# 640 accumulator columns divided into 512 and 128 in place of 320 and 320

## The chip, the cores and the metric

The kernel runs on one core of one Trainium2 chip. The metric is the device time of one execution in microseconds; the time before is the median of three runs. The profile is that of one further execution.

## What is computed

One inference step of a two-layer trunk on 128 context tokens and 512 latent tokens, 640 in all, model width 1024, in float32. The reference, cut to what matters here:

```python
# layer 0: latent attention || windowed attention
h, gate = _adaln(x, ln, mod)                       # RMSNorm, then h*(1+scale)+shift
cq, ckv, krope, z_a, q_b, k_b, v_b, z_b = _split(h @ w_in, L0_SPLIT)
q_a = (_rms(cq, mla_q_norm) @ w_uq)                # 8 heads of 64 + 32 (rotary)
k_a, v_a = _mla_expand(ckv, krope, w_ukv)          # 640 keys for a latent query
o_a = softmax(q_a k_a^T * MLA_SCALE) v_a           # dense
o_b = windowed softmax with sink                   # |i-j| <= 128, plus 128 cached keys
y = concat(o_a * silu(z_a), o_b * silu(z_b)) @ w_out;  x = x + gate * y

# layer 1: bidirectional gated DeltaNet || dense attention
q, k, v = silu(short_conv(qkv))                    # 3 taps along the tokens, 1536 columns
o_f, o_b = chunked delta rule, forward and backward
o_d = softmax(q_d k_d^T * ATT_SCALE) v_d           # 4 heads, 640 keys for a latent query
y = concat(gated GDN output, o_d * silu(z_d)) @ w_out
```

## The kernel before

Every projection is computed in three passes: each operand is kept as a high part and a low part in the type fp32r (`split`, lines 108 to 111: ScalarE writes the high part, VectorE or GpSimd the low one), and `mm3` (lines 113 to 118) issues high*high, then two mixed products, into one PSUM accumulator. A PSUM bank holds 512 float32 columns.

There are two kinds of projection. `proj_tok` (tokens on the partitions of the result) takes one 128-token tile as the stationary operand and streams up to 512 weight columns; the change does not touch it. `proj_col` (lines 191 to 203; the columns of the weight on the partitions, the tokens along the free dimension) holds a 128x128 block of the weight stationary and streams the tokens. 640 tokens do not fit one bank, so there are two accumulators. For each weight unit (four row blocks), the two accumulators are served one after the other, with 4 x 3 matmuls each. `proj_col` is called 13 times in layer 0 (keys and queries of the windowed attention, `use_qk`; the two gates, `use_z` and `z_raw`) and 16 times in layer 1 (twelve column blocks for the short convolution, `use_conv` with `conv`, lines 1026 to 1037, and four gate blocks, `use_zd`).

The same division of 640 stands at four other places: the rotary part of the latent queries (line 569), `heads_q` (line 711, by `col3`), the scores of the latent attention (line 772; 32 tiles of 128 queries by 640 keys, three passes each) and those of the dense attention of layer 1 (line 1380; 16 tiles). `heads_k` (line 723) covers 768 keys in two accumulators of 384. Scores lie in an accumulator `S` of two banks; `softmax` (line 310) takes the maximum on VectorE (line 319) and the exponential on ScalarE (line 321) over all 640.

The order of each engine's instructions is set when the kernel is built: a scheduler goes through the program with a model of durations and writes one fixed order for each engine. Weights come in on SP's queue (`unit`, line 134), in that order too. The modulation vectors are computed by `gemv_mm` (line 228), whose small matmuls (line 236) read `wmod` tiles just loaded and stand between the projections.

Of the kernel before, what the change touches and what calls it, by code (L numbers as in the profile page):

```python
# [22 lines left out]
NT = 5  # L23
EPS = 1e-6
# [8 lines left out]
class Blocks:  # L33
    """row blocks of an operand of 1024 rows, in two tiles"""
# [11 lines left out]
class Kern:  # L46
    def __init__(self, ctx, tc, io):
        self.ctx, self.tc, self.nc, self.io = ctx, tc, tc.nc, io
        self.n = 0
        self.dve_share = 2      # one in so many evacuations goes to VectorE  # L50
# [25 lines left out]
    def banks(self, ctx, **roles):  # L76
        """PSUM banks by role; role "S2" counts accumulators of two banks"""
# [3 lines left out]
        for r in roles:         # banks in the order of the roles  # L81
            self.acc2() if r == "S2" else self.acc1(r)
# [4 lines left out]
    def acc1(self, role="tr"):  # L87
        if role not in self.roles:      # any bank, in turn
            self.nb = getattr(self, "nb", 0) + 1
            role = ("sc", "tr", "sc", "tr", "sc", "o")[self.nb % 6]  # L90
        return self.t(self.ps, [128, 512], role, bufs=self.roles[role])

    def ranked(self, rank):
        """decorator: what the function issues is scheduled that much earlier (or later)"""
# [51 lines left out]
    def unit_in(self, src, raw, hi, lo, eng):  # L146
        """unit in flat views of tiles at hand"""
# [6 lines left out]
    def proj_tok(self, name, n, hT, use, order="k", us=None, pre=None):  # L154
        """[tokens, n] = h @ w for the five token tiles; units hold as many row blocks as fit 4 KB"""
# [35 lines left out]
    def proj_col(self, src, hT, use):  # L191
        """[128 columns, tokens] in two accumulators of 320 tokens; src [2][128, 4, 128]"""
        hh, hl = hT
        us = [self.unit(src[i], [4, 128]) for i in range(2)]
        ps = [self.acc1("pj")[:, 0:320] for _ in range(2)]
        for i in range(2):
            wh, wl = us[i]
            for f in range(2):
                r = slice(f * 320, f * 320 + 320)
# [28 lines left out]
    def gemv_mm(self, m, src, out):  # L228
        """out [128, 256] (PSUM): partial products of both vectors with src [8][128, 512]; rows 32 (2 (k % 2) + f) + group"""
# [9 lines left out]
    def mod_k(self, m, c):  # L239
        """shift and scale of the row blocks 2 c and 2 c + 1"""  # L240
# [10 lines left out]
        # columns of mt: (f = shift | scale, row block, group)  # L251
# [9 lines left out]
    def mod_gate(self, m, c, role="tr"):  # L261
        """gate, columns 512 c .. 512 c + 511, bias included: two summands by group to DRAM"""
# [11 lines left out]
    def gate(self, m, pool, gt=None):  # L274
        """gates of both groups on all partitions"""
# [8 lines left out]
    def xhat(self, x, junk):  # L284
        """normalises x in place"""
# [7 lines left out]
    def norm_T(self, t, x, m, hT, th):  # L293
        """transposed, modulated x (normalised) of token tile t"""
# [15 lines left out]
    def softmax(self, S, shape, pool, scale, l, tag="P"):  # L310
        """S: PSUM view [128, ...]; returns P in SBUF, flat [128, n], not normalised; sums into the column l"""
# [12 lines left out]
    def factors(self, L, rd, pool, tag="rB", bufs=1):  # L324
        """1 / L [128 tokens, heads x tiles], one row per head, on all partitions of the head's columns; rd [heads x tiles, 128]"""
# [15 lines left out]
    def gated(self, o, z, ts):  # L341
        """gate the values o[:, 0:n] of tokens ts"""
# [11 lines left out]
    def layer0(self, m0, m1):  # L354
# [21 lines left out]
        # normalised, transposed input; modulated row block by row block as the modulation vectors come in  # L376
        xT = [self.t(sw, [128, 4, NTOK], "g10", bufs=2) for _ in range(2)]
        # tiles of later use serve as further buffers here
# [25 lines left out]
        # small operands  # L404
# [20 lines left out]
        def modulate(k):  # L425
            """row block k of the modulated input"""
# [45 lines left out]
        def use_qk(j):  # L472
            def use(ps):
                X = self.t(tmp, [128, NTOK], "tX", bufs=3)
                for f in range(2):
                    self.evac(X[:, f * 320:f * 320 + 320], ps[f])
# [27 lines left out]
        # per key head: both parts of the queries, against keys of which both halves hold the same part  # L504
# [48 lines left out]
        def use_z(z, j):  # L553
            def use(ps):
                for f in range(2):
                    nc.scalar.activation(out=z[:, j, f * 320:f * 320 + 320], in_=ps[f], func=AF.Silu)
# [4 lines left out]
        # ---- rotary part of the latent queries  # L561
# [1132 lines left out]
```

## Time and profile before

| | |
|---|---|
| time, median of 3 runs | 919.71 us (915.09 to 920.54) |
| profiled execution: span from first to last instruction | 909.3 us |
| PE (TensorE matmul) busy | 839.4 us, 92% of the span, 5762 matmuls |
| PEld (weight loads) busy | 708.0 us, 78%, 5762 loads |
| DVE / ACT / POOL busy | 559.9 us (62%) / 374.3 us (41%) / 291.0 us (32%) |
| mean granted TensorE clock | 0.962 |

The page gives no time of the profiled execution beside its span; the median of the timed runs lies 10.4 us above the span, which is what lies before the first and behind the last instruction, and the difference between executions. In the rows of the timeline the columns are the start in us, the duration in us, the engine, the line, the operation, what it writes and reads, the shape and the count. For a matmul the shape names the stationary operand (128\*128) and the result (128x320: 128 partitions, 320 columns). The duration of a single matmul contains the way through the array, so the cost of one in a sequence is read from the distance of two starts, not from its duration.

### The profile page before, as it was taken

The numbers are of one execution on the slowest core, as the hardware profiler recorded it, in microseconds if no ns is written. First come the engines' busy times: TensorE is split into PE (matmuls) and PEld (weight loads), VectorE is DVE, ScalarE is ACT, GpSimd is POOL, SyncE is SP. The second block draws the span as 40 slices with busy tenths as digits, with TensorE's granted clock in tenths as the row PEclk, the third lists the DMA queues.
The fourth block names the chain that finished last, engine by engine and source line by source line (L and its number), as shares of the span: only waits on it lengthen the run. The fifth ranks groups of instructions, "written<-read, shape, count | busy, mean of one in ns | idle before, by whom it ended". The sixth has DMA issues, their size and how long they took to land.

```text
span 909.3 us, 15742 instructions
## 1 busy us (share of the span) xinstructions
PE 839.4 (92%) x5762; PEld 708.0 (78%) x5762; DVE 559.9 (62%) x1260; ACT 374.3 (41%) x916; POOL 291.0 (32%) x398
## 2 busy tenths in 40 slices
PE   5999899989999999999999799999788799999996
PEld 3579779977868776688888679888688688988785
DVE  4546545266476676524986646756997357887634
ACT  5234423345476566513445525342232323456330
POOL 2013434220141013243672101032995012145441
PEclk9899999999999999999999899999898769999999
DMA  9875894230270111364933545449205913346512
GB/s 315 308 230 137 221 305 121 85 82 15 67 188 16 30 30 43 101 235 138 218 111 98 172 139 148 111 148 250 58 25 134 267 52 107 112 123 212 185 47 93
DMA packets 100935, 124.46 MB, mean 137 GB/s; under 512 B 20014, under 2 KB 60698, under 8 KB 100602
## 3 DMA queue, kind: packets, MB, share of 16 engines
q1 hardware_dynamic: 97418, 115.60, 42.8%
q0 software_dynamic: 2720, 5.25, 2.7%
q10 hardware_dynamic: 720, 2.62, 0.7%
q8 instruction: 45, 0.74, 0.3%
q14 instruction: 32, 0.26, 0.1%
HBM read 100.48 MB, written 20.39 MB: 133 GB/s over the span
## 4 chain that ended last, share of the span: by engine, by line
PE 67%; DVE 12%; DMA 10%; ACT 4%; issue 3%; POOL 2%; SPq 1%; DVEq 0%; ACTq 0%; POOLq 0%
PE pj L116 10%; PE pj L117 10%; PE pj L118 10%; PE tr L122 6%; PE S L772 3%; PE o L796 2%; DVE Ub L1167 2%; DVE wb L1165 2%; PE tr L236 2%; PE S L1380 1%; PE o L659 1%; PE sc L1282 1%; DMA wmod<-in_w_mod 1%; PE sc L1230 1%; PE sc L117 1%
## 5 line engine op out<-in xcount | busy, mean ns | idle before, releaser
L110 ACT ACTIVATE whi<-wraw 128x512 fp32r<-128x512 f32 (+4 forms) x113 | 75.1, 666 | 184.0 <-PE pj L118 53.1
L111 DVE TENSOR_TENSOR wlo<-wraw,whi 128x512 fp32r<-128x512 f32 (+3 forms) x76 | 59.6, 785 | 79.6 <-ACT whi L110 77.6
L111 POOL TENSOR_TENSOR wlo<-wraw,whi 128x512 fp32r<-128x512 f32 (+4 forms) x37 | 50.9, 1375 | 142.7 <-ACT whi L110 121.9
L116 PE MATMUL pj<-hUh,whi 128*128 128x320 f32 x256 | 81.8, 319 | 0.8 <-DVE Ub L1167 0.6
L118 PE MATMUL pj<-hUh,wlo 128*128 128x320 f32 x256 | 81.3, 317 | 1.3 <-DVE wlo L111 1.3
L117 PE MATMUL pj<-hUl,whi 128*128 128x320 f32 x256 | 81.5, 318 | 0.0
L116 PE MATMUL pj<-hTh,whi 128*128 128x320 f32 x208 | 66.2, 318 | 3.9 <-ACT whi L110 3.9
L117 PE MATMUL pj<-hTl,whi 128*128 128x320 f32 x208 | 66.1, 318 | 0.0
L118 PE MATMUL pj<-hTh,wlo 128*128 128x320 f32 x208 | 65.7, 316 | 0.0
L116 PE MATMUL pj<-whi,hUh 128*128 128x512 f32 (+2 forms) x160 | 57.1, 358 | 9.1 <-DVE t L931 6.1
L117 PE MATMUL pj<-wlo,hTh 128*128 128x512 f32 (+1 forms) x160 | 59.5, 374 | 0.0
L319 DVE TENSOR_REDUCE smx<-S 128x1 f32<-128x640 f32 (+1 forms) x60 | 42.6, 713 | 26.3 <-PE S L772 10.5
L116 PE MATMUL pj<-whi,hTh 128*128 128x512 f32 (+1 forms) x160 | 57.7, 374 | 0.9 <-ACT Xs L131 0.9
L118 PE MATMUL pj<-whi,hTl 128*128 128x512 f32 (+1 forms) x160 | 57.2, 368 | 0.0
L118 PE MATMUL pj<-whi,hUl 128*128 128x512 f32 (+2 forms) x160 | 55.9, 352 | 0.4 <-DVE hUl L111 0.4
L321 ACT ACTIVATE P<-S,smx 128x640 f32<-128x640 f32 (+1 forms) x60 | 42.4, 708 | 33.0 <-DVE smx L320 31.3
L117 PE MATMUL pj<-wlo,hUh 128*128 128x512 f32 (+2 forms) x160 | 55.8, 349 | 0.0
L116 PEld LDWEIGHTS pj<-hUh,whi 128*128 128x128 f32 x256 | 49.2, 192 | 5.8 <-issue 4.5
L118 PEld LDWEIGHTS pj<-hUh,wlo 128*128 128x128 f32 x256 | 49.4, 193 | 2.0 <-DVE wlo L111 1.6
L117 PEld LDWEIGHTS pj<-hUl,whi 128*128 128x128 f32 x256 | 49.2, 192 | 1.3 <-issue 1.2
L116 PEld LDWEIGHTS pj<-hTh,whi 128*128 128x128 f32 x208 | 39.7, 191 | 5.7 <-ACT whi L110 4.1
L116 PEld LDWEIGHTS pj<-whi,hUh 128*128 128x128 f32 x160 | 31.8, 199 | 13.1 <-DVE t L931 6.6
(529 smaller groups left out, 2249.8 us busy)
## 6 DMA issues: line engine op xcount, KB each, us to landing
Pw<-in_w_mod SPq DMA_DIRECT2D x48, 256.0 KB
wraw<-in_w1c SPq DMA_DIRECT2D x32, 256.0 KB
wraw<-in_w_out SPq DMA_DIRECT2D x16, 512.0 KB
wraw<-in_w0c SPq DMA_DIRECT2D x26, 256.0 KB
zB<-in_w_mod SPq DMA_DIRECT2D x16, 256.0 KB
zA<-in_w_mod SPq DMA_DIRECT2D x16, 256.0 KB
wmod<-in_w_mod SPq DMA_DIRECT2D x16, 256.0 KB
ut_d<-zt SPq DMA_DIRECT2D x10, 258.0 KB
```

What stands on the lines that cost most here:

```text
L110: self.last_hi = nc.scalar.activation(out=hi, in_=src, func=AF.Copy)
L111: (lo_eng or nc.vector).tensor_tensor(out=lo, in0=src, in1=hi.bitcast(F32), op=ALU.subtract)
L116: nc.tensor.matmul(out, ah, bh, start=start, stop=False)
L117: nc.tensor.matmul(out, ah, bl, start=False, stop=False)
L118: nc.tensor.matmul(out, al, bh, start=False, stop=stop)
L122: self.nc.tensor.transpose(out, in_, self.ident[:p, :p])
L236: nc.tensor.matmul(out[32 * g:32 * g + 32, 0:256], self.sc[:, k, :], raw[:, f * 256:(f + 1) * 256], start=(k < 2), stop=(k >= 6), tile_pos ...
L319: nc.vector.tensor_reduce(out=m, in_=src, axis=AX.X if len(shape) == 1 else AX.XY, op=ALU.max)
L321: nc.scalar.activation(out=Pv, in_=src, func=AF.Exp, bias=nm, scale=scale, accum_out=l)
L772: nc.tensor.matmul(S[:, f, 0:320], Qe[:, a, qs], Ke[:, b, 128 + 320 * f:448 + 320 * f], start=(a + b == 0), stop=(a == 1))
L796: nc.tensor.matmul(o[rr[e], 0:256], V[:, 1 + s, hc[e]], x[:, e * 256:(e + 1) * 256], start=(s == 0), stop=(s == 4), tile_position=(0, 64 * e))
L1165: eng.tensor_tensor(out=w, in0=Ub[:, r, c:c + 1].to_broadcast([80, nr, nn]), in1=Lb[d][:, c:c + 1, cc].to_broadcast([80, nr, nn]), op=ALU. ...
```

## The change

640 tokens or keys are divided into 512 and 128. In the column projections, `SEG` serves the 512 latent tokens (128 to 639) first and the 128 context tokens behind them. In the scores the first 512 keys fill one bank of `S` and the other 128 the start of the next, so that the 640 scores lie contiguous. `heads_k` divides its 768 into 512 and 256. `conv` copies its input with two instructions in place of three, since the boundary of the segments is now the boundary between the token groups. The number of matmuls and of multiplied columns stays the same. The rest of the diff removes comments.

```diff
+SEG = (slice(128, 640), slice(0, 128))
...
     def proj_col(self, src, hT, use):
         us = [self.unit(src[i], [4, 128]) for i in range(2)]
-        ps = [self.acc1("pj")[:, 0:320] for _ in range(2)]
+        ps = [self.acc1("pj")[:, 0:r.stop - r.start] for r in SEG]
         for i in range(2):
             wh, wl = us[i]
-            for f in range(2):
-                r = slice(f * 320, f * 320 + 320)
+            for f, r in enumerate(SEG):
                 for k in range(4):
                     kk = 4 * i + k
                     self.mm3(ps[f], (wh[:, k, :], wl[:, k, :]), (hh[:, kk, r], hl[:, kk, r]), kk == 0, kk == KD - 1)
...
-                    self.evac(X[:, f * 320:f * 320 + 320], ps[f])
+                    self.evac(X[:, SEG[f]], ps[f])
...
-            for f in range(2):
-                r = slice(f * 320, f * 320 + 320)
-                ps = self.acc1("pj")[:, 0:320]
+            for r in SEG:
+                ps = self.acc1("pj")[:, 0:r.stop - r.start]
...
-        def col3(w, cols, x, nk, half, use, wide=False):
+        def col3(w, cols, x, nk, segs, use, wide=False):
-            for f in range(2):
+            for r in segs:
...
-            col3(uk, slice(j * 128, j * 128 + 128), ckT, 2, 384, use_k, j == 0)
+            col3(uk, slice(j * 128, j * 128 + 128), ckT, 2, (slice(0, 512), slice(512, 768)), use_k, j == 0)
...
-                        S = self.acc2()
+                        S = self.acc2().rearrange("p a b -> p (a b)")
                         for (a, b) in ((0, 0), (0, 1), (1, 0)):
                             for f in range(2):
-                                nc.tensor.matmul(S[:, f, 0:320], Qe[:, a, qs], Ke[:, b, 128 + 320 * f:448 + 320 * f],
+                                nc.tensor.matmul(S[:, 512 * f:512 + 128 * f], Qe[:, a, qs], Ke[:, b, 128 + 512 * f:640 + 128 * f],
                                                  start=(a + b == 0), stop=(a == 1))
-                        Ps[q, e] = self.softmax(S[:, :, 0:320], [2, 320], pp, MLA_SCALE, Ls[j % 2][:, NT * e + q + 1:NT * e + q + 2])
+                        Ps[q, e] = self.softmax(S[:, 0:640], [640], pp, MLA_SCALE, Ls[j % 2][:, NT * e + q + 1:NT * e + q + 2])
...
         def conv(ps, c):
-            nc.scalar.copy(xp[:, 1:129], ps[0][:, 0:128])
-            nc.vector.tensor_copy(xp[:, 130:322], ps[0][:, 128:320])
-            nc.scalar.copy(xp[:, 322:642], ps[1])
+            nc.scalar.copy(xp[:, 130:642], ps[0])
+            nc.vector.tensor_copy(xp[:, 1:129], ps[1])
...
-                        nc.tensor.matmul(S[:, f, 0:320], qD[a][:, h, qs], kD[b][:, g, 128 + 320 * f:448 + 320 * f],
+                        nc.tensor.matmul(S[:, 512 * f:512 + 128 * f], qD[a][:, h, qs], kD[b][:, g, 128 + 512 * f:640 + 128 * f],
                                          start=(a + b == 0), stop=(a == 1))
-                Ps.append(self.softmax(S[:, :, 0:320], [2, 320], pp, ATT_SCALE, L[:, 1 + q:2 + q]))
+                Ps.append(self.softmax(S[:, 0:640], [640], pp, ATT_SCALE, L[:, 1 + q:2 + q]))
```

The scheduler writes new orders with it. The line numbers of the changed kernel lie one above or below those of before (`mm3` is lines 117 to 119, a load line 107, the scores of the latent attention line 771). Two places follow.

On PE, the first scores of the latent attention (tile `S`) stood before as six equal matmuls, two accumulators in each of three passes:

```order
L118 MATMUL pj_3299<-cqTh_248,hTh_529_2696 128x320
L772 MATMUL S_628_3123<-K_537_2716,Q_533_2712 128x320 x6
```

Now they alternate between 512 and 128 columns:

```order
L771 MATMUL S_628_3123<-K_537_2716,Q_533_2712 128x512
L771 MATMUL S_628_3123<-K_537_2716,Q_533_2712 128x128
L771 MATMUL S_628_3123<-K_537_2716,Q_533_2712 128x512
L771 MATMUL S_628_3123<-K_537_2716,Q_533_2712 128x128
L771 MATMUL S_628_3123<-K_537_2716,Q_533_2712 128x512
L771 MATMUL S_628_3123<-K_537_2716,Q_533_2712 128x128
```

So no two long matmuls follow each other within a tile of scores; in the column projections 12 or 24 long ones are followed by as many short ones.

On SP, in layer 1 between the first column projections, the loads of `wmod` (modulation), of `wraw` (weights) and the store and re-load of the decay exponents (`gc_d`, then `Dm` on all partitions) stood before in this order:

```order
L106 DMA wmod_5489<-in_w_mod 128x512
L106 DMA wmod_5493<-in_w_mod 128x512
L106 DMA wraw_5878<-in_w1c 128x512
L106 DMA gc_d_4840<-gcT_5175 40x128
L106 DMA Dm_5178<-gc_d_4840 128x5x128 x2
L106 DMA Dm_5192<-gc_d_4840 128x5x128 x2
L106 DMA wmod_5497<-in_w_mod 128x512
```

They now stand in this one (the numbers of the `wmod` and `wraw` tiles are three to six lower in the changed kernel):

```order
L107 DMA gc_d_4840<-gcT_5175 40x128
L107 DMA wmod_5486<-in_w_mod 128x512
L107 DMA Dm_5178<-gc_d_4840 128x5x128 x2
L107 DMA Dm_5192<-gc_d_4840 128x5x128 x2
L107 DMA wmod_5490<-in_w_mod 128x512
L107 DMA wraw_5872<-in_w1c 128x512
```

The store of the exponents has moved ahead of two modulation loads and one weight load, and its re-load ahead of one of each.

More of the change, by code (lines that the diff above doesn't have):

```diff
@@ L555, in use @@
                 for f in range(2):
-                    nc.scalar.activation(out=z[:, j, f * 320:f * 320 + 320], in_=ps[f], func=AF.Silu)
+                    nc.scalar.activation(out=z[:, j, SEG[f]], in_=ps[f], func=AF.Silu)
             return use
@@ L678, in use @@
                 for f in range(2):
-                    self.evac(zA[:, j, f * 320:f * 320 + 320], ps[f])
+                    self.evac(zA[:, j, SEG[f]], ps[f])
             self.proj_col(io["w0c"][9 + j], hT, use)
@@ L701, in mla_setup @@
                 self.load(K[b][1][32:64], krd, nc.gpsimd)
-        def col3(w, cols, x, nk, half, use, wide=False):
-            for f in range(2):
-                ps = (self.acc2()[:, 0, 0:half] if wide else self.acc1("pj")[:, 0:half])
+        def col3(w, cols, x, nk, segs, use, wide=False):
+            for r in segs:
+                n = r.stop - r.start
+                ps = (self.acc2()[:, 0, 0:n] if wide else self.acc1("pj")[:, 0:n])
                 for k in range(nk):
-                    r = slice(f * half, f * half + half)
                     self.mm3(ps, (w[0][:, k, cols], w[1][:, k, cols]), (x[0][:, k, r], x[1][:, k, r]), k == 0, k == nk - 1)
-                use(slice(f * half, f * half + half), ps)
+                use(r, ps)
         def heads_q(j):
@@ L718, in use_q @@
                     self.split(ps[p], Qj[e][p, 0, r], Qj[e][p, 1, r])
-            col3(uq[j // 2], slice((j % 2) * 128, (j % 2) * 128 + 128), cqT, 3, 320, use_q, j == 0)
+            col3(uq[j // 2], slice((j % 2) * 128, (j % 2) * 128 + 128), cqT, 3, SEG, use_q, j == 0)
             for e in range(2):
@@ L1194, in use @@
                 for f in range(2):
-                    nc.scalar.activation(out=zz[:, f * 320:f * 320 + 320], in_=ps[f], func=AF.Silu)
+                    nc.scalar.activation(out=zz[:, SEG[f]], in_=ps[f], func=AF.Silu)
                 self.load(zd_d[j], zz)
@@ L1375, in scores @@
             for q in range(4):
-                S = self.acc2()
+                S = self.acc2().rearrange("p a b -> p (a b)")
                 qs = slice(128 + 128 * q, 256 + 128 * q)
```

## The prediction

> **What bounds the kernel now.** I read the busy times first, then the chain that ended last, then the table of stages, then starts in the timeline.
>
> ```profile
> PE 839.4 (92%) x5762; PEld 708.0 (78%) x5762; DVE 559.9 (62%) x1260; ACT 374.3 (41%) x916; POOL 291.0 (32%) x398
> PE 67%; DVE 12%; DMA 10%; ACT 4%; issue 3%; POOL 2%; SPq 1%; DVEq 0%; ACTq 0%; POOLq 0%
> PE pj L116 10%; PE pj L117 10%; PE pj L118 10%; PE tr L122 6%; PE S L772 3%; PE o L796 2%; DVE Ub L1167 2%; DVE wb L1165 2%; PE tr L236 2%; PE S L1380 1%; PE o L659 1%; PE sc L1282 1%; DMA wmod<-in_w_mod 1%; PE sc L1230 1%; PE sc L117 1%
> ```
>
> TensorE is busy for 92% of the span and carries 67% of the chain; the three lines of `mm3` alone carry 30%. PEld has as many weight loads as there are matmuls: no load is shared, also where two matmuls in a row have the same stationary operand. The average hides stages with other limits, so here are the stages that hold affected matmuls (start:end, length, then PE, PEld, DVE, ACT and POOL busy, clock, DMA share, GB/s):
>
> ```profile
> 96.00:275.00 179.00, 169.20 (x1193) 143.35 (x1194) 94.39 (x223) 79.67 (x203) 49.62 (x48) 0.99 0.47 132
> 275.00:375.00 100.00, 98.55 (x660) 75.78 (x658) 65.70 (x148) 60.04 (x138) 20.97 (x17) 1.00 0.09 28
> 450.00:510.00 60.00, 49.89 (x338) 43.99 (x337) 45.97 (x124) 29.36 (x83) 26.75 (x59) 0.94 0.48 133
> 510.00:545.00 35.00, 35.00 (x242) 29.63 (x241) 17.12 (x28) 13.55 (x35) 4.43 (x13) 1.00 0.45 135
> 545.00:585.00 40.00, 38.04 (x251) 36.40 (x250) 27.18 (x66) 18.23 (x42) 5.75 (x14) 1.00 0.45 130
> 625.00:716.00 91.00, 77.94 (x541) 71.00 (x539) 74.83 (x182) 25.34 (x81) 61.67 (x112) 0.91 0.47 118
> 716.00:830.00 114.00, 107.63 (x1101) 97.87 (x1102) 80.08 (x201) 47.12 (x136) 30.84 (x28) 0.88 0.39 113
> ```
>
> From 96 to 375 us PE is busy for 95% of the time or more, and from 510 to 545 us without a gap. Two stages are different, as the chain cut to 450 to 510 us and to 625 to 716 us shows:
>
> ```profile
> by line: DMA wmod<-in_w_mod 16.2%; issue 15.6%; POOL t L942 5.9%; PE pj L236 5.3%; POOL t L932 4.5%; POOL th L306 4.2%; PE pj L117 3.9%; PE pj L116 3.8%; DVE wlo L111 3.7%; PE pj L118 3.4%; DVE t L1035 3.4%; PE tr L122 2.5%; POOL ssq L128 2
> by line: DVE Ub L1167 23.7%; DVE wb L1165 23.1%; SPq L106 6.4%; DMA Dm<-L_d 5.3%; DMA U<-ut_d 5.2%; DMA ut_d<-LA 4.5%; DVE wlo L111 4.5%; issue 4.4%; DVE t L940 3.7%; DVE t L931 3.3%; DMA wraw<-in_w1c 2.8%; PE pj L116 1.5%; DVE vDl L111 1.5
> ```
>
> In the first, `mm3` has 11% of the chain, between DMA and the normalisation on POOL; in the second the inversion of the blocks on DVE (L1165, L1167) holds 47%. PE idles 10.1 and 13.1 us there.
>
> **What one pair costs.** The change replaces each pair of 320-column matmuls by one of 512 and one of 128. The number of instructions and of columns stays, so everything hangs on the cost of a matmul by its length. In an undisturbed column projection of before, the first and the last of 24:
>
> ```profile
> 182.96 0.31 PE L116 MATMUL pj<-hTh,whi 128*128 128x320 f32 x1
> ...
> 186.33 0.31 PE L118 MATMUL pj<-hTh,wlo 128*128 128x320 f32 x1
> ```
>
> 23 distances in 3.37 us: 147 ns for 320 columns. In a token projection, the first and the last of 20 with 512 columns:
>
> ```profile
> 399.69 0.39 PE L117 MATMUL pj<-wlo,hTh 128*128 128x512 f32 x1
> ...
> 404.00 0.39 PE L118 MATMUL pj<-whi,hTl 128*128 128x512 f32 x1
> ```
>
> 19 distances in 4.31 us: 227 ns. Short ones of the same type stand in the scores of the context tokens and between long ones in the mask of the windowed attention:
>
> ```profile
> 302.13 0.28 PE L117 MATMUL S<-K,Q 96*128 96x128 f32 x1
> 302.24 0.27 PE L118 MATMUL S<-K,Q 96*128 96x128 f32 x1
> ...
> 181.60 0.39 PE L621 MATMUL S<-kB0h,g 128*128 128x512 f32 x1
> 181.82 0.33 PE L623 MATMUL S<-mask,identR 128*128 128x128 f32 x2
> 181.99 0.45 PE L624 MATMUL S<-kB0l,g 128*128 128x512 f32 x1
> 182.28 0.40 PE L621 MATMUL S<-kB1h,g 128*128 128x512 f32 x1
> ```
>
> The first two rows lie 110 ns apart. From 181.60 to 182.28 two matmuls of 512 and two of 128 take 0.68 us; less 2 x 227 this leaves 113 ns for a short one, in company of long ones. From 320 to 512 columns a column costs (227 - 147) / 192 = 0.42 ns, which would make 128 columns 67 ns. The short ones cost 112: something other than the streaming of columns sets their pace, and with one weight load for each matmul I take it for that load, which 147 ns of streaming cover and 67 do not. A new pair then costs 227 + 112 = 339 ns where the old one cost 2 x 147 = 294: **45 ns more for each pair**. Bounds from the rows: 67 ns for the short one gives no change (294), 113 gives 46.
>
> The Trainium skill weighs the other way: its page "TensorE: Matmul & The Clock Gate", section "Back-to-back issue gap", gives an isolated matmul N / 2.4 + 2.5 ns, which counts columns alone: 216 + 56 = 272 ns for the new pair and 2 x 136 = 272 for the old, so a change of nothing. By the rows above it is 45 ns. The trace does not agree with that formula for 128 columns (56 against 112), though the same section warns that it leaves out the weight load.
>
> **How many pairs, and where.** 29 column projections of 24 pairs are 696; the rotary part has 18, `heads_q` 4 x 9 = 36, the scores 32 x 3 = 96 and 16 x 3 = 48: 894 pairs. `heads_k` goes from 384 + 384 to 512 + 256, both long enough, and I cost it at nothing. So PE gets 894 x 45 ns = **40 us** more work. By stage, from the rows of one of the three passes (for 96 to 275, 450 to 510, 510 to 545, 545 to 585, 625 to 716 and 716 to 830 us, the last from a score's pass):
>
> ```profile
> L116 PE MATMUL pj<-hTh,whi 128*128 128x320 f32 x192 | 61.2, 319 | 3.9 <-ACT whi L110 3.9
> L116 PE MATMUL pj<-hUh,whi 128*128 128x320 f32 x70 | 22.6, 323 | 0.2 <-DVE t L931 0.2
> L116 PE MATMUL pj<-hUh,whi 128*128 128x320 f32 x57 | 18.2, 320 | 0.0
> L116 PE MATMUL pj<-hUh,whi 128*128 128x320 f32 x65 | 20.3, 312 | 0.0
> L116 PE MATMUL pj<-hUh,whi 128*128 128x320 f32 x64 | 20.7, 323 | 0.6 <-DVE Ub L1167 0.6
> L1380 PE MATMUL S<-kDh,qDh 128*128 128x320 f32 x30 | 8.9, 380 | 1.5 <-ACT P L321 1.5
> ```
>
> Three passes, two matmuls to a pair: a row of x192 is 288 pairs.
>
> - 96 to 275 us: 288 pairs, with the rotary part and the first `heads_q` some 318: 14.3 us. PE is busy for 169.2 of 179 us, so 95% of it counts: 13.5.
> - 275 to 375 us: 96 pairs of scores and about 23 of `heads_q`: 5.4 us, all of it.
> - 450 to 510 us: 105 pairs, 4.7 us. PE idles 10.1 us for others: 0.
> - 510 to 545 us: 86 pairs, 3.9 us, all.
> - 545 to 585 us: 98 pairs, 4.4 us. PE is nearly full, but the chain also leads through the decay masks; half: 2.2.
> - 625 to 716 us: 96 pairs of the last gate blocks and 3 of scores, 4.5 us, beside the inversion on DVE: 0. If that cover were gone, all 4.5 would count.
> - 716 to 830 us: 45 pairs of scores, 2.0 us, 94% busy: 1.9.
> - The 24 pairs before 96 us (1.1 us) lie where DMA and the modulation decide: 0.
>
> The sum on the path is 13.5 + 5.4 + 3.9 + 2.2 + 1.9 = **27 us**, of 40 us added.
>
> **The other edits.** Copies out of PSUM change size:
>
> ```profile
> L1033 ACT COPY t<-pj 128x320 f32<-128x320 f32 x12 | 5.0, 415 | 0.0
> L1031 ACT COPY t<-pj 128x128 f32<-128x128 f32 x12 | 3.1, 260 | 9.0 <-PE pj L118 8.1 <-DVE sp L996 0.9
> ```
>
> `conv` loses one of three copies, and the copy that comes last behind a projection has 128 columns, 260 ns in place of 415. The large copy runs while the 12 short matmuls stream. This shortens a tail by 0.15 us for 29 blocks, 4 us at most if each tail were on the chain; PE works on the next block meanwhile, so I take 0, and keep -4. The softmax reads the same 640 columns: 0.
>
> The new order on SP lets the store of the decay exponents go out ahead of two `wmod` loads and a weight load. Before, it stood behind a weight load that held the queue for 5 us, and PE then waited for a `wmod` load behind the broadcast:
>
> ```profile
> 485.27 0.80 SPq L106 DMA_DIRECT2D wmod<-in_w_mod  x2
> 490.96 0.33 SPq L106 DMA_DIRECT2D wraw<-in_w1c  x1
> 491.61 0.30 SPq L106 DMA_DIRECT2D gc_d<-gcT  x1
> ...
> 505.98 1.07 PE L236 MATMUL pj<-wmod,sc 128*32 128x256 f32 x4 [5.99 <-DMA wmod<-in_w_mod]
> ```
>
> That wait of 6.0 us may shrink, since the store can leave up to 5.7 us earlier, or stay, since `wmod` still stands behind the broadcast, or grow by as much, as the `wmod` loads are now issued later. Between -6 and +6 I take 0, the middle. On PE `gemv_mm` (L236) stands in the order between projections, and the projections queue behind it.
>
> **The rivals.**
>
> 1. *Nothing soaks up the extra work.* PE's order is fixed, so a delay ahead of a wait can be followed by the same wait if what it waits for was itself fed by PE (the decay masks and the Gram products are). Then all 40 us count: 960. For it: PE busy 92%. Against it: 23 us of idle time in the two stages named.
> 2. *The waits soak up more and the SP order helps.* Half of the 9.8 us of idle time between 96 and 275 us and the half of 545 to 585 us go too, with the 6 us on SP: 27 - 5 - 2 - 6 = 14, so 934.
> 3. *Not slower: the short load hides.* In 12 short matmuls nothing helps, but where a short one stands between long ones its load could come early enough: the two L623 start 220 ns behind L621, and L624 only 170 ns behind them. If the load of the long one hid too, a pair would cost 227 + 67 = 294, the saved tails would be left, and the time would be 916 to 920. The point from which it decides: the start of the long matmul behind a short one, below 100 ns after it. Against it speaks 0.68 us for the four, which holds 113 ns each.
> 4. *Faster: long matmuls stream more cheaply than their columns.* If 512 columns cost what 320 do, a pair would cost 147 + 112 = 259, 35 ns less, 31 us over all pairs: 889. The same section of the Trainium skill gives a sustained 131 ns for 512 columns and 81 for 128, a pair of 212. The row of 227 ns speaks against both.
>
> **How the numbers follow.** Against the profiled span of 909.3 us the sum gives 936; the median of the runs lies 10.4 us above that span, so 919.7 + 27 = **947 us**. Chances: the forecast with its own spread 60%, rival 1 18%, rival 2 15%, rival 3 5%, rival 4 2%. The range reaches to rival 2 and rival 1 with the 2 to 3 us by which runs differ: 932 to 963. About 1% (9 us) is what a measurement here tells from no change. Faster by more than that is rival 4, 2%; within it rival 3 and a little of rival 2, 6%; slower 92%.
>
> **What would show it.** In the profile after: starts 110 to 113 ns apart in the 128-column matmuls of the projections and 225 to 232 in the 512-column ones, scores of six matmuls in 1.02 us of starts where they took 0.88; as many weight loads as matmuls; the stage of the latent attention's scores 5 us longer; the inversion (L1165, L1167) still holding the chain, with PE idle less than 13 us beside it. The prediction is wrong if short matmuls follow at 60 to 70 ns, if the granted clock falls in the projections, or if the waits in layer 1 before the inversion change by more than 6 us.

## The result and the profile after

| | before | after |
|---|---|---|
| time, median of 4 runs each | 917.4 us (914.49 to 920.54) | 954.1 us (949.58 to 958.01) |
| profiled execution: span | 909.3 us | 952.0 us |
| PE busy | 839.4 us | 886.6 us |

The ratio is 1.0409 (95% interval 1.037 to 1.0448): 36.7 us slower. The profiled execution of after took 953.78 us with a span of 952.0, so only 1.8 us lie outside a span. The profiled execution of before must then have taken about 911.1 us, 6.3 less than the median; differences between the two traces (42.7 us in the span) overstate the loss by that much.

From the page of the profile after: busy times, then the chain by engine and by line (`mm3` is now L117 to L119):

```profile
PE 886.6 (93%) x5762; PEld 719.9 (76%) x5762; DVE 562.2 (59%) x1260; ACT 374.7 (39%) x904; POOL 292.7 (31%) x398
PE 60%; DMA 12%; DVE 12%; POOL 6%; issue 5%; ACT 4%; SPq 1%; DVEq 0%; POOLq 0%; ACTq 0%
PE pj L117 8%; PE pj L118 8%; PE pj L119 8%; PE tr L123 6%; PE S L771 3%; PE o L795 2%; PE tr L236 2%; DVE Ub L1165 1%; PE S L1378 1%; PE o L658 1%; DMA wraw<-in_w0c 1%; SPq L107 1%; DVE wb L1163 1%; DMA Dm<-gc_d 1%; DMA wraw<-in_w_out 1%
```

The number of matmuls and weight loads is as before, PE is busy 47 us longer, and yet its share of the chain has fallen from 67 to 60%, while DMA and POOL have gained. So beside the longer matmuls there is something else.

Starts in one column projection of after (start, duration, engine, line, operation, tiles, shapes):

```profile
164.44 0.27 PE L119 MATMUL pj<-hTh,wlo 128*128 128x128 f32 x1
...
165.44 0.28 PE L119 MATMUL pj<-hTh,wlo 128*128 128x128 f32 x1
165.55 0.45 PE L117 MATMUL pj<-hTh,whi 128*128 128x512 f32 x1
165.84 0.40 PE L118 MATMUL pj<-hTl,whi 128*128 128x512 f32 x1
...
168.16 0.39 PE L119 MATMUL pj<-hTh,wlo 128*128 128x512 f32 x1
...
169.67 0.45 PE L117 MATMUL pj<-hTh,whi 128*128 128x512 f32 x1
```

Nine distances from 164.44 to 165.44 are 111 ns each, ten from 165.84 to 168.16 are 232 ns. From one unit to the next (165.55 to 169.67) twelve pairs take 4.12 us, 343 ns each: 49 more than 2 x 147. A tile of scores, six matmuls up to the next instruction, takes 0.99 us where it took 0.88, and the 512 columns behind it take 0.28 (the instruction after them starts at 314.28) where 0.23 is usual; together that is about three pairs of 343 ns:

```profile
313.01 1.16 PE L771 MATMUL S<-K,Q 96*128 96x512 f32 x6
314.00 0.45 PE L119 MATMUL tr<-hTl,ckTl 128*128 128x512 f32 x1
```

To see where the time went, both spans are cut at the same eight events: the first column projection of layer 0, the first score and the last value product of the latent attention, the first column projection of layer 1, the first Gram product, the first and last step of the inversion on DVE, the last column projection, the end. The columns are start:end, length, then PE, PEld, DVE, ACT and POOL busy, clock, DMA share, GB/s. Before:

```profile
67.20:278.70 211.50, 200.72 (x1441) 172.03 (x1440) 116.25 (x272) 94.18 (x244) 61.83 (x69) 0.99 0.48 134
278.70:382.80 104.10, 101.44 (x681) 76.61 (x680) 68.13 (x150) 62.00 (x138) 20.97 (x17) 1.00 0.12 35
382.80:458.60 75.80, 75.37 (x404) 64.49 (x402) 39.96 (x52) 24.82 (x48) 38.55 (x37) 1.00 0.72 194
458.60:545.40 86.80, 77.07 (x518) 66.23 (x518) 56.71 (x144) 38.35 (x102) 26.12 (x65) 0.96 0.44 133
545.40:628.40 83.00, 81.04 (x450) 71.81 (x449) 51.13 (x130) 33.64 (x73) 14.68 (x21) 1.00 0.56 162
628.40:697.40 69.00, 56.70 (x321) 51.52 (x320) 67.93 (x168) 19.37 (x67) 61.67 (x112) 0.88 0.29 72
697.40:709.70 12.30, 12.30 (x88) 12.13 (x87) 2.76 (x7) 1.91 (x4) 0.00 (x0) 1.00 0.94 238
709.70:909.30 199.60, 180.40 (x1525) 156.07 (x1523) 123.80 (x272) 74.85 (x195) 57.43 (x54) 0.91 0.41 129
```

After:

```profile
68.00:292.80 224.80, 214.70 (x1426) 173.93 (x1425) 116.03 (x271) 95.26 (x243) 62.65 (x69) 0.98 0.45 125
292.80:402.30 109.50, 107.35 (x696) 77.43 (x695) 69.22 (x151) 62.57 (x139) 21.02 (x17) 1.00 0.12 36
402.30:478.40 76.10, 75.34 (x404) 64.47 (x402) 40.37 (x52) 24.79 (x48) 38.53 (x37) 1.00 0.69 193
478.40:570.80 92.40, 86.28 (x518) 68.14 (x518) 57.84 (x143) 38.83 (x95) 26.63 (x65) 0.98 0.41 125
570.80:666.20 95.40, 92.61 (x471) 77.25 (x471) 50.52 (x131) 33.74 (x69) 16.66 (x22) 0.98 0.51 144
666.20:737.50 71.30, 55.70 (x309) 48.85 (x307) 68.86 (x169) 19.25 (x67) 59.82 (x111) 0.87 0.27 70
737.50:753.00 15.50, 15.50 (x77) 13.38 (x77) 2.15 (x4) 1.48 (x3) 0.00 (x0) 0.81 0.97 245
753.00:952.00 199.00, 182.71 (x1525) 157.09 (x1524) 123.80 (x272) 73.56 (x195) 57.56 (x54) 0.91 0.38 123
```

In the order of the rows the stretches grow by 13.3, 5.4, 0.3, 5.6, 12.4, 2.3, 3.2 and -0.6 us, and 0.8 us come ahead of the first: 42.7. The largest surprise is the fifth, from the first Gram product to the inversion. It holds 98 pairs, which at 49 ns are 4.8 us, and it grew by 12.4. Two rows of it, in the groups of instructions by shape, are one of the three passes of the token projections `w1z` and `w1q`, which come from behind the inversion in the program. Before:

```profile
L116 PE MATMUL pj<-whi,hUh x56: 388/393/586, 583.1 to 628.4; 128*128 128x512 f32 x56
```

After:

```profile
L117 PE MATMUL pj<-whi,hUh x63: 388/396/628, 612.0 to 666.2; 128*128 128x512 f32 x63
```

Seven more for each pass are 21 matmuls of 232 ns, 4.9 us, that now run ahead of the inversion and no longer under it, where PE idles. The last of the 40 Gram products (`tr<-KQ`) divides the stretch. Up to it, before, after, and in the kernel with layer 1 alone changed, which comes further down:

```profile
545.40:619.10 73.70, 71.74 (x409) 64.25 (x408) 46.23 (x116) 32.38 (x71) 14.68 (x21) 1.00 0.51 151
570.80:655.50 84.70, 81.91 (x424) 68.58 (x424) 45.42 (x116) 31.83 (x66) 15.37 (x21) 0.98 0.46 137
553.40:636.10 82.70, 80.38 (x425) 67.49 (x425) 45.73 (x116) 31.83 (x66) 15.37 (x21) 1.00 0.47 141
```

This part grew by 11.0 us. On PE 141 matmuls of the token projections stand ahead of the last Gram product where 126 did: 15 matmuls, 3.5 us, that the scheduler has moved. With the 4.8 us of the pairs that is 8.3; layer 1 alone, with the same 15, grew by 9.0. After has a granted clock of 0.98 where both others have 1.00: from 634.1 to 637.5 us it was 0.50, and matmuls of 512 columns started 427 ns apart. PE's idle time in the part rose only from 2.0 to 2.8 us. So it is PE's work that made this part longer. Behind the last Gram product 9.3 us became 10.7, and the other six of the 21 matmuls run in that time. The chain of the whole stretch has another owner. Before, then after:

```profile
by line: PE pj L116 15.3%; PE pj L117 15.2%; PE pj L118 14.9%; DMA Dm<-gc_d 7.4%; PE tr L1108 6.8%; DMA Dm<-L_d 5.8%; DVE LA L1117 4.5%; DMA L_d<-LA 3.2%; DVE t L1036 3.0%; DVE Dm L1096 3.0%; PE tr L122 2.8%; issue 2.7%; DVE t L1035 2.4%; A
```

```profile
by line: DMA Dm<-gc_d 12.4%; DMA A_d<-LA 7.7%; PE pj L118 7.5%; DMA L_d<-LA 7.4%; PE pj L117 7.3%; PE pj L119 7.3%; DVE LA L1115 6.5%; SPq L107 5.8%; issue 4.8%; DVE Dm L1094 3.9%; DVE t L1034 3.7%; PE tr L1106 3.7%; DVE LA L1117 2.9%; ACT 
```

The projections held 45% of it and now hold 22%; in their place stand the transfers of the decay masks (`Dm`) and of the blocks built from them (`LA`, stored to `L_d` and `A_d`). The chain follows one of the paths that run side by side here; PE is busy for 92.61 of the 95.40 us all the same.

The experiments ask two things: what a short matmul pays for, and what the new order costs without any longer matmul. Times below are medians; "above before" is against the runs of before on the same chip: 914.25 us for the projections in 512 and 128, 448 and 192, 384 and 256 with the latent end first, and layer 1 alone; 914.94 us for scores alone, long and short in turn, and the two controls of the sequence; 916.57 us for the other four.

### The profile page after: what moved, and what is told of

It reads as the page before. It is cut to its first block, busy times and chain, and to the rows that moved or that the text cites. A ratio compares the mean times of both kernels' runs of the same rounds, so it can differ in the third digit from the quotient of the medians.

```text
span 952.0 us, 15728 instructions
## 1 busy us (share of the span) xinstructions
PE 886.6 (93%) x5762; PEld 719.9 (76%) x5762; DVE 562.2 (59%) x1260; ACT 374.7 (39%) x904; POOL 292.7 (31%) x398
## 4 chain that ended last, share of the span: by engine, by line
PE 60%; DMA 12%; DVE 12%; POOL 6%; issue 5%; ACT 4%; SPq 1%; DVEq 0%; POOLq 0%; ACTq 0%
PE pj L117 8%; PE pj L118 8%; PE pj L119 8%; PE tr L123 6%; PE S L771 3%; PE o L795 2%; PE tr L236 2%; DVE Ub L1165 1%; PE S L1378 1%; PE o L658 1%; DMA wraw<-in_w0c 1%; SPq L107 1%; DVE wb L1163 1%; DMA Dm<-gc_d 1%; DMA wraw<-in_w_out 1%
## 5 line engine op out<-in xcount | busy, mean ns | idle before, releaser
L112 DVE TENSOR_TENSOR wlo<-wraw,whi 128x512 fp32r<-128x512 f32 (+3 forms) x76 | 63.5, 837 | 69.1 <-ACT whi L111 68.8
L117 PE MATMUL pj<-hUh,whi 128*128 128x512 f32 (+1 forms) x256 | 89.4, 349 | 1.1 <-DVE vDl L112 1.1
L119 PE MATMUL pj<-hUh,wlo 128*128 128x512 f32 (+1 forms) x256 | 88.8, 347 | 0.0
L118 PE MATMUL pj<-hUl,whi 128*128 128x512 f32 (+1 forms) x256 | 88.7, 347 | 0.0
L117 PE MATMUL pj<-hTh,whi 128*128 128x512 f32 (+1 forms) x208 | 71.0, 341 | 2.0 <-ACT whi L111 2.0
L119 PE MATMUL pj<-hTh,wlo 128*128 128x512 f32 (+1 forms) x208 | 70.7, 341 | 0.0
L118 PE MATMUL pj<-hTl,whi 128*128 128x512 f32 (+1 forms) x208 | 70.5, 339 | 0.0
L117 PE MATMUL pj<-whi,hUh 128*128 128x512 f32 (+2 forms) x160 | 57.8, 364 | 10.6 <-DVE t L930 5.3
L117 PE MATMUL pj<-whi,hTh 128*128 128x512 f32 (+1 forms) x160 | 59.0, 377 | 0.0
L117 PEld LDWEIGHTS pj<-hUh,whi 128*128 128x128 f32 x256 | 50.6, 198 | 9.6 <-issue 2.4
L119 PE MATMUL pj<-whi,hTl 128*128 128x512 f32 (+1 forms) x160 | 57.4, 368 | 0.0
L119 PE MATMUL pj<-whi,hUl 128*128 128x512 f32 (+2 forms) x160 | 56.6, 356 | 0.4 <-DVE hUl L112 0.4
L119 PEld LDWEIGHTS pj<-hUh,wlo 128*128 128x128 f32 x256 | 50.2, 196 | 5.9 <-issue 0.5
L117 PEld LDWEIGHTS pj<-hTh,whi 128*128 128x128 f32 x208 | 40.1, 193 | 7.2 <-ACT whi L111 2.3
L119 PEld LDWEIGHTS pj<-hTh,wlo 128*128 128x128 f32 x208 | 40.0, 193 | 5.9 <-issue 1.2
```

What stands on the lines that cost most here:

```text
L112: (lo_eng or nc.vector).tensor_tensor(out=lo, in0=src, in1=hi.bitcast(F32), op=ALU.subtract)
L117: nc.tensor.matmul(out, ah, bh, start=start, stop=False)
L118: nc.tensor.matmul(out, ah, bl, start=False, stop=False)
L119: nc.tensor.matmul(out, al, bh, start=False, stop=stop)
```

## What a short matmul pays for

**Column projections alone.** `SEG` with 512 and 128 in the column projections, the rotary part and `heads_q` (750 pairs); scores and `heads_k` as before.

```diff
-                for (a, b) in ...: nc.tensor.matmul(S[:, 512 * f:512 + 128 * f], ...)
+                for (a, b) in ...: nc.tensor.matmul(S[:, f, 0:320], ...)
```

> The 512 + 128 division in the column projections, the rotary part and heads_q alone (750 pairs); scores and heads_k as before. Theory A (each short matmul takes the 112 ns of its weight load, so a pair costs 343 ns in place of 294, and nothing soaks it up): 750 x 0.045 to 0.049 = 34 to 37 us over the kernel before. Theory B (waits of layer 1 soak up what falls there, as forecast): 13.5 + 3.9 + 2.2 = about 20 us. Theory C (it is not the short matmul but the new order of the schedule or the uneven copies): no fixed number, but then a milder uneven division costs much the same.

Measured: 947.49 us, 33.2 above before (ratio 1.0367, 1.0329 to 1.0405). The column projections carry nearly all of the loss, at 44 ns a pair.

**448 and 192.** The same kernel with another boundary:

```diff
-SEG = (slice(128, 640), slice(0, 128))
+SEG = (slice(192, 640), slice(0, 192))
```

> As proj512, but divided into 448 and 192. 192 columns stream in about 93 ns, still below the 112 ns of a weight load; 448 columns take about 200 ns. Theory A: a pair costs 312 ns, 18 more than before, 750 x 0.018 = 13 to 14 us over the kernel before, and starts of the 192-column matmuls 110 to 113 ns apart. Theory C: about as much as proj512. If columns alone counted: no change.

Measured: 927.81 us, 13.6 above (1.0141, 1.0112 to 1.017). Matmuls of 192 columns in its timeline:

```profile
194.50 0.27 PE L121 MATMUL pj<-hTh,wlo 128*128 128x192 f32 x1
...
194.83 0.27 PE L121 MATMUL pj<-hTh,wlo 128*128 128x192 f32 x1
```

Three distances are 0.33 us: 110 ns, the price of 128 columns. So there is a floor. What sets it, the next three kernels ask.

**Half the streaming.** The changed kernel, with 64 columns in place of 128 in the mixed products of the context tokens:

```diff
-    nc.tensor.matmul(ps[f], w[:, k, :], x[:, kk, r], ...)
+    nc.tensor.matmul(ps[f][:, 0:64], w[:, k, :], x[:, kk, 0:64], ...)
```

> The changed kernel, but of the 24 short matmuls of a column projection the 16 mixed products stream 64 columns in place of 128 (left out: the mixed products of the context tokens 64 to 127); the number of matmuls and of weight loads stays. 464 matmuls are half as long. Theory A (the weight load, not the streaming, paces the short ones at 112 ns): as the changed kernel, 35 to 40 us above before, starts still 109 to 114 ns apart. Theory S (streaming paces them, 0.42 ns a column): 27 ns less for each, starts near 85 ns, 12 us faster than the changed kernel at most.

Measured: 953.24 us, 36.7 above (1.0414, 1.0369 to 1.0459): no gain at all over the 36.7 of the whole change.

```profile
182.76 0.31 PE L210 MATMUL pj<-hTh,whi 128*128 128x128 f32 x1
182.90 0.24 PE L210 MATMUL pj<-hTl,whi 128*128 128x64 f32 x1
182.98 0.28 PE L210 MATMUL pj<-hTh,wlo 128*128 128x64 f32 x1
183.09 0.30 PE L210 MATMUL pj<-hTh,whi 128*128 128x128 f32 x1
```

Three matmuls still take 330 ns, 110 each, though two of them stream half. (The single distances of 140, 80 and 110 show that a start may be put down a little early and the next one made up for it; only a sum over a group is to be trusted.) Streaming does not pace them.

**Half the load.** The same products with the first 64 columns of the stationary block, streaming all 128 tokens:

```diff
-    nc.tensor.matmul(ps[f], w[:, k, :], x[:, kk, r], ...)
+    nc.tensor.matmul(ps[f][0:64, :], w[:, k, 0:64], x[:, kk, r], ...)
```

> The changed kernel, but the 16 mixed products of a column projection that serve the context tokens use only the first 64 of the 128 columns of their stationary block and stream all 128 tokens (left out: the mixed products of columns 64 to 127 for the context tokens). Theory A (the load of the stationary block paces the short ones, and its time goes with its columns): the starts of these matmuls move from 112 ns toward 67 ns, the price of streaming 128 columns, and the time falls by up to 15 to 20 us against the changed kernel. Theory F (a fixed price of about 112 ns for each matmul, whatever it loads): starts still 109 to 114 ns apart, and the time within 5 us of the changed kernel, apart from what the new order brings.

Measured: 936.34 us, 19.8 above (1.0225, 1.0181 to 1.027), 17 less than the change.

```profile
195.61 0.27 PE L210 MATMUL pj<-hTh,whi 128*128 128x128 f32 x1
195.72 0.22 PE L210 MATMUL pj<-hTl,whi 128*64 128x128 f32 x1
195.78 0.22 PE L210 MATMUL pj<-hTh,wlo 128*64 128x128 f32 x1
195.84 0.27 PE L210 MATMUL pj<-hTh,whi 128*128 128x128 f32 x1
```

Three matmuls take 230 ns where they took 330: 60 ns for each of the two with a half block, 110 for the one with a full block. (The second shape in a row is that of the operand which streams, 128 rows by 128 columns here; the result of a half block has 64 partitions.) That is theory A: the load of the stationary block sets the pace, and it goes with the columns of the block. By rows, a matmul costs the larger of its streaming (0.45 to 0.47 ns a column at 256 to 512 columns) and its load (111 ns for 128 columns). The Trainium skill has a rule for this, on its page "TensorE: Matmul & The Clock Gate", section "LDWEIGHTS (loading the stationary operand)": a load takes its number of columns divided by 1.2, in ns, whatever the rows. That gives 107 ns for 128 columns, with which the 111 here agree, and 53 for 64. Of the 53 the rows show only that such a load takes 60 ns or less: 128 streamed columns at 0.45 to 0.47 ns would take 58 to 60 by themselves (an estimate from the rows).

**Long and short in turn.** Each stationary block serves 512 and then 128 columns:

```diff
-            for f, r in enumerate(SEG):
-                for k in range(4): mm3(ps[f], ...)
+            for k in range(4):
+                for w, x in ((wh, hh), (wh, hl), (wl, hh)):
+                    for f, r in enumerate(SEG): matmul(ps[f], w[:, k, :], x[:, kk, r], ...)
```

> The changed kernel, but in the column projections each stationary block serves 512 and then 128 columns before the next block, so that long and short matmuls alternate; the same 24 + 24 matmuls and loads. Theory A (a short matmul costs its load's 112 ns wherever it stands): as the changed kernel, 35 to 40 us above before, a long and a short start 340 to 344 ns apart. Rival 3 of the prediction (a short one's load hides behind a long one, a pair costs 294): 4 to 10 us above before. Theory C (two matmuls in a row with the same stationary block need only one load): a pair near 231 + 60 = 291 ns, the same as rival 3 in time, but with fewer weight loads than matmuls.

Measured: 952.63 us, 37.7 above (1.0414, 1.0362 to 1.0466). In 453 of its 696 pairs a short one stands between two long ones (the scheduler let runs of one length stand in the others). Six such pairs in the timeline, two matmuls to a row:

```profile
488.14 0.51 PE L203 MATMUL pj<-hUh,whi 128*128 128x512 f32 x2
...
490.20 0.45 PE L203 MATMUL pj<-hUh,whi 128*128 128x512 f32 x1
```

2.06 us for six pairs are 343 ns, the same as in runs. Rival 3, the short load that hides behind a long matmul, is refuted, and so is theory C: the page of this kernel has 5762 loads for 5762 matmuls, so a block that is used twice in a row is loaded twice.

**Scores alone** (144 pairs in both layers, the projections as before):

> 512 and 128 keys in the scores of both layers alone (144 pairs); column projections, rotary part, heads_q and heads_k as before. Theory A (every pair costs 45 to 49 ns and PE is full where they stand): 6 to 7 us above before. Theory B (waits of the softmax stage take half of it): 3 us.

Measured: 923.42 us, 8.5 above (1.0097, 1.0065 to 1.013). Theory A's 6 to 7 lies inside the interval (5.9 to 11.9 us), theory B's 3 outside it. The projections alone and the scores alone add up to 41.7 us, the whole change is 36.7: their intervals leave room for that, and each kernel has an order of its own.

## What the order costs

**384 and 256, the latent end first.** 256 columns still cover their load, so no pair gets dearer:

```diff
-SEG = (slice(128, 640), slice(0, 128))
+SEG = (slice(256, 640), slice(0, 256))
```

> As proj512, but divided into 384 and 256. 256 columns stream in 118 ns, above the 112 ns of a weight load; 384 take 176: 294 ns, the same as two of 320. Theory A: within 1% of the kernel before (0 to 3 us). Theory C: clearly slower, since the division is uneven and the schedule is new.

Measured: 929.15 us, 14.9 above (1.0142, 1.0103 to 1.0182). A miss, although the matmuls cost what was expected; the first and last of 15 distances each, for 384 and for 256 columns:

```profile
184.98 0.33 PE L119 MATMUL pj<-hTh,whi 128*128 128x384 f32 x1
...
187.58 0.33 PE L119 MATMUL pj<-hTh,whi 128*128 128x384 f32 x1
```

```profile
191.46 0.28 PE L120 MATMUL pj<-hTl,whi 128*128 128x256 f32 x1
...
193.26 0.28 PE L120 MATMUL pj<-hTl,whi 128*128 128x256 f32 x1
```

173 and 120 ns, together the old 294, and the kernel is slower all the same. So part of the loss is no matter of the matmul's price, and the agreement of 448 and 192 with its forecast may hold an amount of this too.

**384 and 256, the context first**, and **320 and 320, the latter half first.** The two take apart what the last one changed at once, the lengths and the sequence.

```diff
-SEG = (slice(256, 640), slice(0, 256))
+SEG = (slice(0, 384), slice(384, 640))
```

> The column projections, the rotary part and heads_q in 384 and 256 tokens, the context tokens in the first segment (0 to 383, then 384 to 639), so in the sequence of before; the earlier kernel with the same two lengths served the latent end (256 to 639) first and was 14.9 us slower than before, though 384 columns start 175 ns and 256 columns 119 ns apart there, together the 294 ns of the old pair. Theory P (lengths decide through the distance of starts, and the order that the scheduler wrote for the latent end first cost that kernel its 14.9 us): 0 to 4 us above before. Theory D (dividing unequally costs something that the starts do not show, such as the clock): 12 to 16 us above before again.

```diff
-SEG = (slice(0, 320), slice(320, 640))
+SEG = (slice(320, 640), slice(0, 320))
```

> Two equal segments of 320 tokens as before, but the second half of the tokens (320 to 639) is served first in the column projections, the rotary part and heads_q, and the copies of the convolution follow that sequence. No length changes. Theory P (order costs by itself: on PE five more matmuls of the token projections now stand ahead of the last Gram product, and other rows move with them): 5 to 15 us above before. Theory D (only an unequal division costs): within 3 us of before.

Measured: 918.01 us, 3.1 above (1.0044, 1.0022 to 1.0067), for the first; 919.84 us, 4.9 above (1.0056, 1.0033 to 1.008), for the second. The same lengths in the sequence of before cost 3, not 15 us, and turning the sequence alone costs 5 (the lower edge of theory P's 5 to 15). For this last kernel the stretch from the first Gram product to the inversion took 86.80 us against 83.00 before. Up to the last Gram product it is

```profile
548.90:623.90 75.00, 72.85 (x413) 64.96 (x413) 46.50 (x114) 32.22 (x71) 15.59 (x21) 1.00 0.48 145
```

1.3 us longer than before: 131 matmuls of the token projections stand ahead of that product in place of 126, and five of them are 1.2 us. With the context first at 384 and 256 they are 126 again, and the part takes 73.3 us. The other 2.5 us lie behind the last Gram product, 11.8 us in place of 9.3. The chain of the stretch has after's look: `Dm`, `L_d` and SP's queue in place of the projections.

Waits of SP's queue in that stretch go with it in part (what was waited for: us in total, times, longest). A weight load waits there until the split of an earlier weight (`wlo`) is done, and the stores of the decay blocks stand in the same queue. Before, then after, two rows each:

```profile
SPq L106 <- DVE wlo L111: 9.3, 5, 4.1
SPq L106 <- POOL wlo L111: 8.4, 4, 3.9
```

```profile
SPq L107 <- DVE wlo L112: 23.8, 9, 7.8
SPq L107 <- POOL wlo L112: 13.1, 3, 5.4
```

Together 17.7 and 36.9 us; with the context first at 384 and 256 they are 16.8, with the latter half first 30.4. But the kernel with half the load has 24.8 us of them, and its way from the last Gram product to the inversion takes 9.2 us, no longer than before. So SP's queue is not shown to be the cause of the 1 to 3 us behind the last Gram product, and it was not tried by itself: the order was changed as a whole.

Open, too, is why the latent end first costs 14.9 us at 384 and 256 and 4.9 at 320. Their traces differ by 11.4 us (the profiled execution of the first was the slowest of its four). Of these, 4.2 lie in the last column projections behind the inversion, 16.3 us at a granted clock of 0.80 against 12.1 at 1.00, and 4.0 in the latent attention, where 17 more matmuls stand and the clock was 0.98 against 1.00. Why the clock was lower is not known.

**The two layers apart.** 512 and 128 in layer 1 alone (432 pairs), then in layer 0 alone (462 pairs):

```diff
+        self.seg = SEG1    # layer 1: 512 and 128; layer 0: 320 and 320 (and the reverse)
```

> The 512 + 128 division in layer 1 alone: 16 column projections and the scores of the dense attention (432 pairs); layer 0 as before. Theory A (nothing soaks it up): 432 x 0.045 to 0.049 = 19 to 21 us over the kernel before. Theory B (the waits of layer 1 soak it up, the forecast's terms): 3.9 + 2.2 + 1.9 = 8 us. In the trace, theory A has the stretch from the first column projection of layer 1 to the first block inversion 13 us longer or more, theory B about 6.

> 512 and 128 in layer 0 alone (13 column projections, rotary part, heads_q, scores of the latent attention, heads_k in 512 and 256: 462 pairs); layer 1 as before. The division in layer 1 alone gave 20.1 us. Theory A (the two layers add up to the 37 us of the whole change): 15 to 19 us above before, and from the first column projection of layer 1 on nothing is longer than before. Theory B (layer 1 takes part of it back in its waits): under 12 us.

Measured: 934.38 us, 20.1 above (1.0223, 1.0192 to 1.0253), for layer 1; 935.95 us, 19.4 above (1.0219, 1.0179 to 1.0259), for layer 0, whose trace is at most 1.4 us longer than before in any of the last five stretches. Together 39.5, the whole change 36.7: they add up within their intervals, and theory B falls for both. Layer 1 pays 46.5 ns for each of its pairs, on the whole the full price; by stretches some of it is soaked up and as much is added.

**Short segment first.** The changed kernel with the 128 context tokens ahead of the 512:

```diff
-SEG = (slice(128, 640), slice(0, 128))
+SEG = (slice(0, 128), slice(128, 640))
```

> The changed kernel with the two segments in the other sequence: in the column projections, the rotary part and heads_q the 128 context tokens are served first, then the 512; the scores as in the changed kernel. The same matmuls; on PE 133 matmuls of the token projections stand ahead of the last Gram product, where the changed kernel has 141 and before 126. Theory P (pairs cost 45 to 55 ns each, and the order adds some us where the latent end is served first): 28 to 35 us above before. Theory D (the order adds nothing): 36 to 38 us above before, as the changed kernel. A tail that is longer, since the large copy now comes last, would put it above 38.

Measured: 951.5 us, 34.9 above (1.0385, 1.0328 to 1.0441). It is within both theories' reach by its interval, 30 to 40 us; inconclusive. A tail that grows with a late large copy does not show.

No experiment points to a version faster than before: the two divisions tried with both parts at 256 or above have the same sum of starts, 293 to 294 ns, and the parts of 128 and 192 columns pay the floor.

## Why the prediction was right or wrong

- **The bound: right.** The loss is on PE, in the column projections, in the matmul's distance of starts.
- **A pair at 45 ns more: right, a little low.** 343 against 294 ns, 49 more; 512 columns start 232 apart (forecast 227), 128 columns 111. Its reason, the weight load, was an inference then; the kernels with half the streaming and half the load show it. The formula of the Trainium skill that counts columns alone (page "TensorE: Matmul & The Clock Gate", section "Back-to-back issue gap") gives 56 ns for 128 columns; with a full load for each, 111 were measured here.
- **Layer 0, 13.5 + 5.4 = 18.9: right.** The trace shows 13.3 and 5.4 us in its two stretches, and layer 0 alone costs 19.4. That each of the two parts fits as well is in part luck: 15 matmuls stood in the first stretch before and stand in the second after (1441 and 681, then 1426 and 696).
- **Layer 1, 3.9 + 2.2 + 1.9 = 8: wrong, it is 20.1.** Three terms failed. "545 to 585 us: ... half: 2.2": the stretch from the Gram products to the inversion grew by 12.4. I had taken the decay masks on the chain as a wait that soaks up PE's work; instead PE's work counted in full (4.8 us), 15 other matmuls came ahead of the last Gram product (3.5 us), the granted clock was 0.98 (3.4 us at 0.50, an estimate of 1.7 us), and the way from the last Gram product to the inversion became 1.4 us longer; 1.0 us stays open. "625 to 716 us: ... 0": I let the inversion on DVE cover the whole stage, but 28 matmuls of each pass stood behind its last step, as this row of before shows:

```profile
L116 PE MATMUL pj<-hUh,whi x28: 302/305/314, 697.4 to 709.7; 128*128 128x320 f32 x28
```

  In that tail PE is busy for 12.30 of 12.30 us, 42 pairs at 294 ns. In after some 39 pairs are left there: 13.4 us at 343 ns, 1.1 of the growth of 3.2. The other 2.1 go with the granted clock, 0.81 there in after and 1.00 in before. From 737.5 to 743.3 us it was 0.50, and seven distances in that time are 427 ns each, where 512 columns start 232 apart at 1.00:

```profile
739.91 0.63 PE L119 MATMUL pj<-hUh,wlo 128*128 128x512 f32 x1
...
742.90 0.61 PE L117 MATMUL pj<-hUh,whi 128*128 128x512 f32 x1
```

  The inversion itself took 2.3 us more, which I can't attribute. "716 to 830 us: 1.9" failed the other way: from the last projection to the end nothing is lost (-0.6), since PE's idle time there fell from 19.2 to 16.3 us.
- **450 to 545 us, 0 + 3.9: nearly right.** It grew by 5.6 us for 191 pairs (9.4 us at 49 ns). The wait for the modulation weights soaked up 3.3 of them; it was 6.0 us long:

```profile
PE pj L236 <- DMA wmod<-in_w_mod: 2.7, 1, 2.7
```

- **The other edits at 0: not refuted for the copies and the softmax** (a gain from the shorter tail shows nowhere). The new order was weighed only at one place on SP, at -6 to +6; that is where a step was missing: an order that differs can cost 5 us by itself without any instruction getting longer, by matmuls that move out from under a cover, as the token projections did.
- **Rivals.** Rivals 3 and 4 are refuted by the starts. Rival 1 (all 40 us count) is the nearer in the end: 36.7 us. But not by its mechanism alone; waits did soak up some 6 us (the modulation weights 3.3, the last stage 2.9), and the order and the clock put about as much back: PE idles 3.3 us longer beside the inversion, and is busy 47.2 us longer in all, where 894 pairs at 49 ns are 43.8.
- **The signs: most came, two did not.** The starts, the number of loads, the scores and the latent attention came as named. But PE idles 15.6 us beside the inversion (71.30 less 55.70), not less than 13, since matmuls that filled that time now run ahead of it. And the granted clock fell in projections, to 0.98 before the inversion and 0.81 behind it, which the prediction named as a sign that it is wrong: no term of the sum has the clock.
- **The sum.** 947 was forecast, 954.1 measured, inside the range. The change was forecast as 27 us and is 36.7; the miss is layer 1's, and the total looks closer than that because the median of before fell from 919.7 to 917.4 with a fourth run. The remark that 10.4 us lie outside the span or between executions was half wrong: 1.8 us lie outside, the rest is that the profiled execution of before lay 6.3 us under the median of four, 8.6 under that of three.

## What to carry to other kernels

Read the price of a matmul from starts at each length that occurs, and look for the length below which it stops falling: here 128 to 192 columns cost the same 111 ns as the load of their 128-column block, and 256 already cover it, so a balanced division is free and an unequal one with a part under 256 pays for each pair. A stage whose chain is on another engine covers only the work that really stands beside that engine: cut it at the first and last instruction of the cover before writing a 0. And where a scheduler rewrites the order, a control that changes the sequence alone, with equal lengths, tells what the order costs; here it was about 5 us, and 12 us between two kernels of the same lengths. Read the granted clock of each stretch beside its length: here a lower clock made up 2 of the 3 us that the last projections lost.

## What the runs showed of the hardware that was not expected

A load of half a block (64 of 128 columns) brought a matmul with 128 streamed columns from 111 down to 60 ns, so its streaming alone costs at most that. Two matmuls in a row with the same stationary block paid for two loads, 343 ns for 512 and 128 columns. A start in the timeline may stand early: behind a run of long matmuls the first short one's successor starts only 60 ns after it, and the first long one behind the short ones is followed after 290 ns, with the sum of the pair unchanged. The granted clock fell to 0.50 for 3.4 us and more at places that differ from kernel to kernel, also while PE was busy without a gap (737.5 to 743.3 us in after), and matmuls of 512 columns then started 427 ns apart in place of 232; no run shows what sets it.
